# Griffin-style hybrid block on one core: operand blocks of the gates' Strassen products copied by transfers inside SBUF, and two of the sums T made by one instruction

## The chip, the cores and the metric

The kernel runs on one core of a Trainium2 chip. The metric is the device time of one execution in microseconds (us). TensorE is called PE, VectorE DVE, ScalarE ACT, GpSimd POOL; SP is the engine from whose queue most transfers are issued.

## What is computed

One layer on a stream of 512 tokens by 2048 features, in float32. The part that matters here is the gates: of the combined input projection, the last two blocks of 2048 columns are `gate_attn` and `gate_conv`, whose sigmoids weigh the attention and the convolution branch.

```
    u = rms_norm(h, mix_pre_g[l])
    proj = u @ w_in[l]
    q, k, v, ca, cb, ga, gb = jnp.split(proj, split_pts, axis=-1)
    ...
    merged = jax.nn.sigmoid(ga) * y_attn + jax.nn.sigmoid(gb) * y_conv
    h = h + rms_norm(merged @ w_out[l], mix_post_g[l])
```

## The kernel before

Tokens lie along the free dimension (NT = 512), features on the 128 partitions; the 2048 features of `u` are 16 tiles of 128x512. Each float32 operand is held as a rounded high part and a low rest (`un0h`, `un0l` and so on), and a product is the sum of three matmuls: high by low, high by high, low by high.

The stages run in program order: convolution inputs, values, queries and keys with attention (8 heads), the gates, layer norm, the output projections, then the feed-forward part. PE, ACT, DVE, POOL and SP each have a queue that is worked in order; a scheduler fixed that order when the kernel was built, and waits between the queues are semaphores.

The gates have 16 output tiles each. The first two of each come by plain products: the loop over `c` (0 to 7) takes one weight chunk of 128x1024 (`raw_g0_c`, split by ACT into `whi_g0_c`, line 124, and by DVE into `wlo_g0_c`, line 125) and issues 24 matmuls (lines 534 to 536) into the four PSUM banks `g0_0` to `g0_3`. The other 14 come by Strassen's scheme with Winograd's sums (`strassen`), which needs other operands: the blocks `b` of `u` (feature tile `c` for "11", tile `c + 8` for "21" and "22"), high part beside low part in one tile of 128x512, and the four sums T1 to T4, again as high beside low. The same loop over `c` makes them, beside the matmuls:

- `un` (line 537): high plus low of feature tile `c` on POOL and of tile `c + 8` on DVE, 128x512 each, into one buffer `un{c}`.
- `b` (lines 542 and 543): per `c` three blocks; the high half of each is copied by ACT, the low half by POOL, 128x256 each. That is 24 copies on ACT and 24 on POOL.
- `tt` (lines 192 to 195, `winograd_t`): the four sums on DVE, 128x256 each. T2 (line 193) needs T1 (line 192), T4 (line 195) needs T2.
- `t12`, `t34` (lines 146 and 147, `merged`): the high part of each sum on ACT, the low part on DVE, four pairs per `c`.

`un` and `tt` share a pool of two buffers, taken in turn. So `un{c+1}` starts when the last sum of `c` (line 195) has been read out of `un{c}`, and `tt{c+1}` starts when all four pairs of `c` are done. The blocks and sums go into a pool of 66 slots of 128x512, in which the slots of finished tiles are used again.

After the loop ACT loads the sigmoid's table and applies it to the four banks (line 555). The first Strassen product, `g2`, accumulates in the bank that the first sigmoid sets free (line 237, then line 239), with `b00` to `b07` as its moving operand. Its weights (`g2q`, `g2s`, `g3q`, `g3s`, lines 217 and 250) are loaded through SP's queue; a weight buffer is loaded anew when DVE has read it, so SP waits for `wlo_g0_4` to `wlo_g0_7` in between.

Of the kernel before, what the change touches and what calls it, by code (L numbers as in the profile page):

```python
# [25 lines left out]
F32 = mybir.dt.float32  # L26
F32R = mybir.dt.float32r
AF = mybir.ActivationFunctionType
ALU = mybir.AluOpType
# [33 lines left out]
def hybrid_block(ctx: ExitStack, tc, xT, vecs, rpb, mask, w_c0, w_qk, w_v, w_gg, w_cg, w_ao, w_co, w_out, w_g0, w_gu, w_dn, outT):  # L63
    nc = tc.nc
# [12 lines left out]
    A, B = slice(0, HN), slice(HN, NT)  # L77

    def slot(name, dt=F32, shape=(P, NT)):
        return sp.tile(list(shape), dt, tag="slot", name=name)  # L80
# [35 lines left out]
    def wchunk(src, name, parts=1):  # L116
        w = src.shape[-1]
        raw = wp.tile([P, 1024], F32, tag="raw", name=f"raw_{name}", bufs=6)[:, :w]
        hi = wp.tile([P, 1024], F32R, tag="whi", name=f"whi_{name}")[:, :w]
        lo = wp.tile([P, 1024], F32R, tag="wlo", name=f"wlo_{name}")[:, :w]  # L120
        for n in range(parts):
            s = slice(n * w // parts, (n + 1) * w // parts)
            nc.sync.dma_start(raw[:, s], src[:, s])
            nc.scalar.copy(hi[:, s], raw[:, s])  # L124
            nc.vector.tensor_tensor(out=lo[:, s], in0=raw[:, s], in1=hi[:, s].bitcast(F32), op=ALU.subtract)  # L125
        taps(rate)
        return hi, lo
# [15 lines left out]
    def merged(src, name):  # L143

        t = slot(name, F32R)
        nc.scalar.copy(t[:, A], src)
        nc.vector.tensor_tensor(out=t[:, B], in0=src, in1=t[:, A].bitcast(F32), op=ALU.subtract)
        return t
# [41 lines left out]
    def winograd_t(u1, u2, t12, t34):  # L190

        nc.vector.tensor_tensor(out=t12[:, A], in0=u1[:, B], in1=u1[:, A], op=ALU.subtract)
        nc.vector.tensor_tensor(out=t12[:, B], in0=u2[:, B], in1=t12[:, A], op=ALU.subtract)
        nc.vector.tensor_tensor(out=t34[:, A], in0=u2[:, B], in1=u1[:, B], op=ALU.subtract)
        nc.vector.tensor_tensor(out=t34[:, B], in0=u2[:, A], in1=t12[:, B], op=ALU.subtract)

    def operands(b11, b2, t12, t34):
        return {
            "11": b11,
            **{n: [t[i] for t in b2] for i, n in enumerate(("21", "22"))},  # L200
            **{n: [t[i] for t in t12] for i, n in enumerate(("T1", "T2"))},
            **{n: [t[i] for t in t34] for i, n in enumerate(("T3", "T4"))},
        }
# [203 lines left out]
    un = []  # L407
# [20 lines left out]
    for half in range(2):  # L428
        rate = R_V[half]
        pv = [(bank, abank)[half](f"pv{half}_{t}") for t in range(NB)]  # L430
        for c in range(HT):
# [3 lines left out]
            for k in range(2):  # L435
                s = slice(k * NT, (k + 1) * NT)
                kt = c * 2 + k
                ah, al = u[kt]
# [88 lines left out]
    for c in range(HT):  # L527
        hi, lo = wchunk(w_gg[c], f"g0_{c}")
        un = stp.tile([P, 2, NT], F32, tag="S", name=f"un{c}")
        for j, k in enumerate((c, c + HT)):  # L530
            ah, al = u[k]
            for n, ps in enumerate(pg):
                s = slice((j * 4 + n) * P, (j * 4 + n + 1) * P)
                nc.tensor.matmul(ps, hi[:, s], al, start=c + j == 0, stop=False)
                nc.tensor.matmul(ps, hi[:, s], ah, start=False, stop=False)
                nc.tensor.matmul(ps, lo[:, s], ah, start=False, stop=c + j == HT)
            (nc.gpsimd, nc.vector)[j].tensor_tensor(
                out=un[:, j], in0=ah.bitcast(F32), in1=al.bitcast(F32), op=ALU.add
            )
            blocks = [slot(f"b{j}{c}_{n}", F32R) for n in range(1 + j)]  # L540
            for t, cols in zip(blocks, (A, B)):
                nc.scalar.copy(t[:, A], ah[:, cols].bitcast(F32))
                nc.gpsimd.tensor_copy(t[:, B], al[:, cols].bitcast(F32))
            if j:
                b2.append(blocks)
            else:
                b11.append(blocks[0])
        tt = stp.tile([P, 2, NT], F32, tag="S", name=f"tt{c}")
        winograd_t(un[:, 0], un[:, 1], tt[:, 0], tt[:, 1])
        t12.append([merged(tt[:, 0, cols], f"t12{c}_{n}") for n, cols in enumerate((A, B))])  # L550
        t34.append([merged(tt[:, 1, cols], f"t34{c}_{n}") for n, cols in enumerate((A, B))])
    for i in range(2):
# [10 lines left out]
    op = operands(b11, b2, t12, t34)  # L563
# [69 lines left out]
    f, acc = [], None  # L633
# [38 lines left out]
    for c in (*range(SPLIT), *range(HT)):  # L672
        if len(w) == c:
            w.append(wchunk(w_g0[0, c], f"f0_{c}"))
            u += [(slot(f"u2_{i}h", F32R), slot(f"u2_{i}l", F32R)) for i in (2 * c, 2 * c + 1)]
            cols = A if c < SPLIT else slice(0, NT)
        else:
            cols = B
# [12 lines left out]
    for j in range(3):  # L691
        t = stp.tile([P, 2, NT], F32, tag="S", name=f"sg{j}")
        t, up = t[:, 0], t[:, 1]
# [10 lines left out]
    for c in range(HT):  # L704
        hi, lo = wchunk(w_g0[1, c], f"f1_{c}")
        for k in range(2):
            i = 2 * c + k
            nc.vector.scalar_tensor_tensor(out=f[i], in0=f[i], scalar=col(C_FPRE, i), in1=r3, op0=ALU.mult, op1=ALU.mult)
            if i < HT:
                moving = [merged(f[i][:, cols], f"b1{i}_{n}") for n, cols in enumerate((A, B))]  # L710
                b11.append(moving[0])
            else:
                moving = [merged(f[i][:, cols], f"b2{i}_{n}") for n, cols in enumerate((A, B))]
                b2.append(moving)
            for n in range(4):
                s = slice((k * 4 + n) * P, (k * 4 + n + 1) * P)
                for m, cols in enumerate((A, B)):
                    plain(pf[n][:, cols], hi[:, s], lo[:, s], moving[m], i + m == 0, i == KT - 1)
            if i >= HT:
                t12, t34 = slot(f"t12_{i}"), slot(f"t34_{i}")  # L720
                winograd_t(f[i - HT], f[i], t12, t34)
                b_t12.append([merged(t12[:, cols], f"t12{i}_{n}") for n, cols in enumerate((A, B))])
                b_t34.append([merged(t34[:, cols], f"t34{i}_{n}") for n, cols in enumerate((A, B))])
    for j in range(2):
        t = slot(f"sg{3 + j}")
# [5 lines left out]
    op = operands(b11, b2, b_t12, b_t34)  # L731
# [6 lines left out]
    for j in range(5, FT):  # L738
# [5 lines left out]
        t, up = slot(f"sg{j}"), slot(f"su{j}")  # L744
# [53 lines left out]
    for i in range(0, KT - 4, 4):  # L798
        t = stp.tile([P, 4, HN], F32, tag="S" if i else "S1", name=f"ha{i}")
        nc.gpsimd.dma_start(t, h_d[i : i + 4, :, A].rearrange("k p t -> p k t"))  # L800
        ha += [t[:, m] for m in range(4)]
    for i in range(KT - 4, KT, 2):
        t = stp.tile([P, 2, HN], F32, tag="quad", name=f"ha{i}", bufs=3)
# [111 lines left out]
```

## Time and profile before

| | |
|---|---|
| median of 3 runs | 2588.96 us (2587.96 to 2590.28) |
| the profiled execution: its time | 2587.58 us |
| the profiled execution: its span | 2585.8 us |
| mean granted clock of TensorE | 0.991 |
| DVE busy in the span | 68% |
| ACT busy in the span | 42% |
| POOL busy in the span | 10% |
| last matmul of the last head's attention starts | 496.63 us |
| the 8 turns of the loop over `c` on DVE (line 195 of turn 0 to line 195 of turn 7) | 496.4 to 540.0 us |
| first matmul of the first Strassen product | 542.58 us |

A row of the time line has the start in us, the duration in us, the engine, line, operation, tile written and tiles read, the count, and in brackets the idle time before it with what ended it. Durations include the pipeline's tail: DVE instructions of 128x256 that follow each other closely last 0.41 to 0.42 us but start 0.33 to 0.34 us apart. [...]

### The profile page before, as it was taken

Reading aid. Unit: us, or ns where it says so; the run is one execution under the profiler, and the core shown is the slowest. Engines: PE = TensorE matmul, PEld = TensorE weight load, DVE = VectorE, ACT = ScalarE, POOL = GpSimd, SP = SyncE. Lnnn points to the kernel's source line nnn. Section 1 sums busy time; section 2 is a strip of 40 time slices with the busy share of each in tenths; the row PEclk is TensorE's granted clock in tenths of the full one; section 3 lists DMA queues with packets and bytes.
Section 4 is the critical chain, followed back from the end, with each engine's and each line's share of the span. In section 5 each row is a group of like instructions: output and inputs, shape, how many; then the busy total and the mean of one; then the engine's idle time right before and its main releaser. Section 6 shows DMA issues by size and latency. Waiting matters only on the chain.

```text
span 2585.8 us, 33614 instructions
## 1 busy us (share of the span) xinstructions
PE 2535.4 (98%) x13078; PEld 2168.7 (84%) x13078; DVE 1751.2 (68%) x2224; ACT 1079.6 (42%) x1560; POOL 263.9 (10%) x290
## 2 busy tenths in 40 slices
PE   9999999989999999998999999999999999999996
PEld 8888888778888888887998888888888878888886
DVE  5999896687776655338888888888788832233336
ACT  5223333455554422224555555555555532233222
POOL 0110222320000011004100000000000100010003
PEclk9999999989999999999999999999999999999998
DMA  6234323356667435234356656656655653353334
GB/s 215 93 127 148 108 95 104 109 149 189 184 189 251 143 129 189 95 104 151 107 158 182 173 172 180 179 171 173 185 169 168 206 174 103 94 170 98 96 97 136
DMA packets 124624, 385.42 MB, mean 149 GB/s; under 512 B 14256, under 2 KB 21552, under 8 KB 124464
## 3 DMA queue, kind: packets, MB, share of 16 engines
q1 hardware_dynamic: 96464, 311.47, 37.0%
q0 software_dynamic: 13024, 45.62, 8.7%
q10 hardware_dynamic: 14976, 26.19, 2.8%
q8 instruction: 102, 1.67, 0.3%
q14 instruction: 58, 0.48, 0.1%
HBM read 350.72 MB, written 32.51 MB: 148 GB/s over the span
## 4 chain that ended last, share of the span: by engine, by line
PE 92%; DVE 4%; issue 2%; ACT 1%; DMA 1%; POOL 1%; POOLq 0%; DVEq 0%; ACTq 0%; SPq 0%
PE f L237 19%; PE f L239 10%; PE g L237 7%; PE pd L170 5%; PE pd L173 5%; PE pd L174 5%; PE g L239 3%; PE po L173 2%; PE po L174 2%; PE po L170 2%; PE qk L174 2%; PE qk L173 2%; PE qk L170 2%; PE py L170 2%; PE py L174 2%; PE py L173 2%
## 5 line engine op out<-in xcount | busy, mean ns | idle before, releaser
L125 DVE TENSOR_TENSOR wlo_wd<-raw_wd,whi_wd 128x1024 fp32r<-128x1024 f32 (+1 forms) x90 | 102.3, 1136 | 283.7 <-ACT whi_wd L124 283.7
L124 ACT CAST whi_wd<-raw_wd 128x1024 fp32r<-128x1024 f32 (+1 forms) x90 | 88.4, 982 | 312.8 <-PE pd L173 306.8
L376 DVE SCALAR_TENSOR_TENSOR cv<-z,vec,cv 128x497 f32<-128x497 f32 (+14 forms) x240 | 190.9, 797 | 4.7
L125 DVE TENSOR_TENSOR wlo_wo<-raw_wo,whi_wo 128x1024 fp32r<-128x1024 f32 x36 | 47.4, 1318 | 106.9 <-ACT whi_wo L124 106.9
L124 ACT CAST whi_wo<-raw_wo 128x1024 fp32r<-128x1024 f32 x36 | 37.9, 1054 | 130.0 <-PE po L173 122.7
L124 ACT CAST whi_y<-raw_y 128x1024 fp32r<-128x1024 f32 x32 | 33.5, 1052 | 78.8 <-PE py L173 75.5
L124 ACT CAST whi_qk<-raw_qk 128x1024 fp32r<-128x1024 f32 x32 | 33.6, 1051 | 77.1 <-PE qk L173 52.7
L125 DVE TENSOR_TENSOR wlo_qk<-raw_qk,whi_qk 128x1024 fp32r<-128x1024 f32 x32 | 40.4, 1261 | 32.3 <-ACT whi_qk L124 32.1
L125 DVE TENSOR_TENSOR wlo_y<-raw_y,whi_y 128x1024 fp32r<-128x1024 f32 x32 | 52.2, 1634 | 10.7 <-ACT whi_y L124 9.5
L616 DVE TENSOR_TENSOR gg<-py,gg 128x512 f32<-128x512 f32 x32 | 21.8, 690 | 53.1 <-PE py L174 53.1
L294 POOL TENSOR_TENSOR r_r<-r_v,mhalf 128x2 f32<-128x2 f32 (+1 forms) x6 | 7.7, 1283 | 458.2 <-DVE r_v L292 458.2
L735 POOL DMA_DIRECT2D ad<-a_d x44 | 24.0, 555 | 262.4 <-PE pd L170 197.6
L170 PE MATMUL py<-ycl,whi_y 128*128 128x512 f32 x128 | 49.8, 389 | 0.0
L173 PE MATMUL py<-ych,whi_y 128*128 128x512 f32 x128 | 49.8, 389 | 0.0
L174 PE MATMUL py<-ych,wlo_y 128*128 128x512 f32 x128 | 49.8, 389 | 0.0
L747 ACT ACTIVATE sg<-sg 128x512 f32<-128x512 f32 x39 | 24.7, 634 | 50.2 <-DVE sg L275 50.2
L455 POOL TENSOR_TENSOR bm<-braw,msk 128x128 f32<-128x128 f32 x56 | 43.0, 801 | 14.0 <-DMA braw<-in_rpb 13.9
L153 PE MATMUL f<-b,whi_f 128*128 128x256 f32 x128 | 36.2, 283 | 0.0
L154 PE MATMUL f<-b,wlo_f 128*128 128x256 f32 x128 | 36.2, 283 | 0.0
L152 PE MATMUL f<-b,whi_f 128*128 128x256 f32 x128 | 36.2, 283 | 0.0
L626 POOL TENSOR_TENSOR gg<-gg,gg 128x512 f32<-128x512 f32 x16 | 21.7, 1355 | 111.2 <-ACT whi_y L124 69.6
L124 ACT CAST whi_ca<-raw_ca 128x1024 fp32r<-128x1024 f32 x12 | 12.6, 1053 | 47.2 <-PE cb L173 19.0
(3045 smaller groups left out, 8284.4 us busy)
## 6 DMA issues: line engine op xcount, KB each, us to landing
raw_wd<-in_w_dn SPq DMA_DIRECT2D x60, 512.0 KB, 3.5
raw_wo<-in_w_out SPq DMA_DIRECT2D x36, 512.0 KB, 3.8
raw_qk<-in_w_qk SPq DMA_DIRECT2D x32, 512.0 KB, 3.7
raw_wd<-in_w_dn SPq DMA_DIRECT2D x30, 384.0 KB, 3.1
a_d<-sg ACTq DMA_DIRECT2D x44, 256.0 KB, 3.7
ad<-a_d POOLq DMA_DIRECT2D x44, 256.0 KB, 4.8
raw_v<-in_w_v SPq DMA_DIRECT2D x16, 512.0 KB, 4.4
raw_y<-in_w_ao SPq DMA_DIRECT2D x16, 512.0 KB, 3.7
```

What stands on the lines that cost most here:

```text
L124: nc.scalar.copy(hi[:, s], raw[:, s])
L125: nc.vector.tensor_tensor(out=lo[:, s], in0=raw[:, s], in1=hi[:, s].bitcast(F32), op=ALU.subtract)
L152: nc.tensor.matmul(o, hi, t[:, B], start=first, stop=False, skip_group_check=True)
L153: nc.tensor.matmul(o, hi, t[:, A], start=False, stop=False, skip_group_check=True)
L154: nc.tensor.matmul(o, lo, t[:, A], start=False, stop=last, skip_group_check=True)
L170: mmul = nc.tensor.matmul(ps, hi[:, s], al, start=first, stop=False)
L173: nc.tensor.matmul(ps, hi[:, s], ah, start=False, stop=False)
L174: nc.tensor.matmul(ps, lo[:, s], ah, start=False, stop=last)
L237: nc.tensor.matmul(ps, hi[:, ws[k]], t, start=first and k == 0, stop=False, skip_group_check=True)
L239: nc.tensor.matmul(ps[:, A], lo[:, ws[k]], t[:, A], start=False, stop=last and k == HT - 1, skip_group_check=True)
L376: nc.vector.scalar_tensor_tensor(out=a[:, to], in0=z[:, fr], scalar=col(C_WDW, i * CW + w), in1=a[:, to], op0=ALU.mult, op1=ALU.add)
L455: nc.gpsimd.tensor_tensor(out=bm[:, o + i - i0], in0=raw[:, :, i * BC : (i + 1) * BC], in1=msk[:, o + i - i0, None, :].broadcast_to([P, RO ...
```

## The change

In the gates' stage, the 48 copies into the blocks `b` are no longer instructions of ACT and POOL but transfers from SBUF to SBUF, issued from SP, 128x256 float32 (128 KB) each. The tile is allocated as float32 and read as `F32R` afterwards. T1 and T3 are made by one DVE instruction of 128x2x256 (`winograd_tt`, line 200 of the changed kernel), T2 and T4 as before (lines 201 and 202). The second place where the four sums are made (the feed-forward stage) keeps `winograd_t`.

```
+    def winograd_tt(un, tt):
+
+        left = un.rearrange("p k (h t) -> p (k h) t", h=2)
+        nc.vector.tensor_tensor(out=tt[:, :, A], in0=left[:, 1::2], in1=left[:, 0:2], op=ALU.subtract)
+        nc.vector.tensor_tensor(out=tt[:, 0, B], in0=un[:, 1, B], in1=tt[:, 0, A], op=ALU.subtract)
+        nc.vector.tensor_tensor(out=tt[:, 1, B], in0=un[:, 1, A], in1=tt[:, 0, B], op=ALU.subtract)
...
-            blocks = [slot(f"b{j}{c}_{n}", F32R) for n in range(1 + j)]
+            blocks = [slot(f"b{j}{c}_{n}") for n in range(1 + j)]
             for t, cols in zip(blocks, (A, B)):
-                nc.scalar.copy(t[:, A], ah[:, cols].bitcast(F32))
-                nc.gpsimd.tensor_copy(t[:, B], al[:, cols].bitcast(F32))
+                nc.sync.dma_start(t[:, A], ah[:, cols].bitcast(F32))
+                nc.sync.dma_start(t[:, B], al[:, cols].bitcast(F32))
+            blocks = [t.bitcast(F32R) for t in blocks]
...
-        winograd_t(un[:, 0], un[:, 1], tt[:, 0], tt[:, 1])
+        winograd_tt(un, tt)
```

The order of PE's instructions is the same in both kernels. On the other engines the order moves in this stage alone. Lines from 196 on have numbers higher by 7 in the changed kernel up to the copies (537 is 544, 542 and 543 are 549 and 550), and by 8 behind them.

On DVE, in turns 0 and 1 (`t120` and `t340` are the pairs of turn 0, `t121` and `t341` those of turn 1), before:

```order
L537 TENSOR_TENSOR un1_4111<-un9h_1608,un9l_1609 128x512
L147 TENSOR_TENSOR t120_0_4093<-tt0_4088,t120_0_4093 128x256
L147 TENSOR_TENSOR t120_1_4096<-tt0_4088,t120_1_4096 128x256
L147 TENSOR_TENSOR t340_0_4099<-tt0_4088,t340_0_4099 128x256
L147 TENSOR_TENSOR t340_1_4102<-tt0_4088,t340_1_4102 128x256
L192 TENSOR_TENSOR tt1_4147<-un1_4111 128x256
L194 TENSOR_TENSOR tt1_4147<-un1_4111 128x256
L193 TENSOR_TENSOR tt1_4147<-un1_4111,tt1_4147 128x256
L195 TENSOR_TENSOR tt1_4147<-un1_4111,tt1_4147 128x256
L125 TENSOR_TENSOR wlo_g0_4_4284<-raw_g0_4_4282,whi_g0_4_4283 128x1024
```

and in the changed kernel:

```order
L544 TENSOR_TENSOR un1_4110<-un9h_1608,un9l_1609 128x512
L125 TENSOR_TENSOR wlo_g0_4_4280<-raw_g0_4_4278,whi_g0_4_4279 128x1024
L147 TENSOR_TENSOR t120_0_4092<-tt0_4088,t120_0_4092 128x256
L147 TENSOR_TENSOR t120_1_4095<-tt0_4088,t120_1_4095 128x256
L147 TENSOR_TENSOR t340_0_4098<-tt0_4088,t340_0_4098 128x256
L147 TENSOR_TENSOR t340_1_4101<-tt0_4088,t340_1_4101 128x256
L200 TENSOR_TENSOR tt1_4146<-un1_4110 128x2x256
L201 TENSOR_TENSOR tt1_4146<-un1_4110,tt1_4146 128x256
L147 TENSOR_TENSOR t121_0_4150<-tt1_4146,t121_0_4150 128x256
L202 TENSOR_TENSOR tt1_4146<-un1_4110,tt1_4146 128x256
```

The rest of weight chunk 4 has moved ahead of the pairs of turn 0 and with it, on ACT, the cast that it waits for.

On POOL, around turn 3, before:

```order
L537 TENSOR_TENSOR un3_4229<-un3h_1282,un3l_1283 128x512
L543 CAST b03_0_4243<-un3l_1283 128x256
L543 CAST b13_0_4259<-un11l_1656 128x256
L543 CAST b13_1_4260<-un11l_1656 128x256
L537 TENSOR_TENSOR un4_4288<-un4h_1508,un4l_1509 128x512
```

and in the changed kernel:

```order
L544 TENSOR_TENSOR un3_4226<-un3h_1282,un3l_1283 128x512
L544 TENSOR_TENSOR un4_4284<-un4h_1508,un4l_1509 128x512
L544 TENSOR_TENSOR un5_4342<-un5h_1514,un5l_1515 128x512
L544 TENSOR_TENSOR un6_4400<-un6h_1555,un6l_1556 128x512
L544 TENSOR_TENSOR un7_4458<-un7h_1561,un7l_1562 128x512
```

Nothing but the `un` sums is left on POOL from turn 2 to turn 7.

On SP, the queue of transfers, in the changed kernel (`g3q` are the weights of the second Strassen tile; before, no other transfer stood between them):

```order
L224 DMA g3q_4712<-in_w_cg 128x1024
L549 DMA b04_0_4298<-un4h_1508 128x256
L550 DMA b04_0_4298<-un4l_1509 128x256
L549 DMA b14_0_4314<-un12h_1696 128x256
L550 DMA b14_0_4314<-un12l_1697 128x256
L549 DMA b14_1_4315<-un12h_1696 128x256
L550 DMA b14_1_4315<-un12l_1697 128x256
L549 DMA b05_0_4356<-un5h_1514 128x256
L550 DMA b05_0_4356<-un5l_1515 128x256
L549 DMA b15_0_4372<-un13h_1702 128x256
L550 DMA b15_0_4372<-un13l_1703 128x256
```

The 48 transfers stand behind `g3s` in the queue: 12, then the third `g2q`, 6, the fourth `g2q`, 6, the first `g3q`, 12, the second `g3q`, 12, and then the last two `g3q`.

## The prediction

> **What bounds the kernel now.** I read the page first, then the list of PE's waits in the gates' stage, the busy times by stretch, and the time line of each engine there.
>
> ```profile
> span 2585.8 us, 33614 instructions
> PE 92%; DVE 4%; issue 2%; ACT 1%; DMA 1%; POOL 1%; POOLq 0%; DVEq 0%; ACTq 0%; SPq 0%
> ```
>
> PE carries 92% of the chain that ended last, so the change, which touches no matmul, can only act where PE waits. In the window of the gates' loop the list of waits (engine, line, waited for: us, times, longest) has four:
>
> ```profile
> PE g L237 <- ACT gs L555: 4.6, 1, 4.6
> PE g L536 <- DVE wlo_g L125: 4.0, 1, 4.0
> PE g L237 <- ACT g2h L232: 1.6, 1, 1.6
> PE po L501 <- DVE ptl L499: 1.1, 1, 1.1
> ```
>
> The first is the end of the loop: PE has finished its plain products and waits for the first sigmoid to free a bank. The second is in mid-loop: the rest of weight chunk 5 comes late from DVE. They look like two gains, but are one. The rows of PE show the pace:
>
> ```profile
> 514.98 0.39 PE L535 MATMUL g<-un5h,whi_g 128*128 128x512 f32 x1
> 519.36 0.80 PE L536 MATMUL g<-un5h,wlo_g 128*128 128x512 f32 x1 [3.99 <-DVE wlo_g L125]
> 526.91 0.39 PE L534 MATMUL g<-un6l,whi_g 128*128 128x512 f32 x1
> 532.35 0.39 PE L534 MATMUL g<-un7l,whi_g 128*128 128x512 f32 x1
> 542.58 2.90 PE L237 MATMUL g<-b,g2h 128*128 128x512 f32 x6 [4.63 <-ACT gs L555]
> ```
>
> One turn is 24 matmuls in 532.35 - 526.91 = 5.44 us, 0.227 us each. Without the wait at 515 the 70 matmuls that are left would end at 515.2 + 70 x 0.227 = 531.1 instead of 537.9, and PE would then wait longer for the same sigmoid. So the start of `g2` at 542.58 is set by what leads to that sigmoid, and that is the loop on DVE with POOL's `un` and ACT's casts:
>
> ```profile
> core 0: us, PE busy (x) PEld busy (x) DVE busy (x) ACT busy (x) POOL busy (x), PEclk, DMA share, GB/s
> 496.39:540.03 43.64, 37.57 (x155) 30.31 (x153) 39.37 (x70) 23.70 (x61) 29.29 (x34) 0.92 0.33 89
> 538.00:542.60 4.60, 0.02 (x1) 0.05 (x1) 4.60 (x11) 3.53 (x7) 0.00 (x0) 0.89 0.01 2
> 540.54 1.28 ACT L555 ACT_TABLE_LOAD   x1
> 541.84 1.09 ACT L555 ACTIVATE gs<-g 128x512 f32<-128x512 f32 x2
> ```
>
> From the last sum of turn 0 to that of turn 7 DVE is busy 39.4 of 43.6 us: it is the bound of the loop. Behind it stand the last casts, the table load (1.28) and one sigmoid, a tail of 542.58 - 540.03 = 2.55 us that the change leaves as it is.
>
> **Why DVE is that busy.** Its instructions are stretched:
>
> ```profile
> L147 DVE TENSOR_TENSOR t<-tt,t 128x256 fp32r<-128x256 f32 x32 | 19.6, 655 | 1.7 <-ACT t L146 1.7
> L147 DVE TENSOR_TENSOR t<-tt,t x32: 411/418/2122, 498.8 to 540.6; 128x256 fp32r<-128x256 f32 x32
> L194 DVE TENSOR_TENSOR tt<-un 128x256 f32<-128x256 f32 x8 | 3.7, 465 | 0.0
> L195 DVE TENSOR_TENSOR tt<-un,tt 128x256 f32<-128x256 f32 x8 | 3.3, 417 | 0.0
> ```
>
> The same shape takes 411 ns at best and 655 ns in the mean of line 147: 32 x 0.244 = 7.8 us lost there alone, and about 1.4 more in lines 192 to 194. What runs on POOL meanwhile tells the cause:
>
> ```profile
> 498.21 0.39 POOL L543 CAST b<-un0l 128x256 fp32r<-128x256 f32 x1
> 498.85 3.34 DVE L147 TENSOR_TENSOR t<-tt,t 128x256 fp32r<-128x256 f32 x4 [1.74 <-ACT t L146]
> 513.10 0.58 DVE L192 TENSOR_TENSOR tt<-un 128x256 f32<-128x256 f32 x1 [1.18 <-POOL un L537]
> 513.35 1.13 POOL L543 CAST b<-un11l 128x256 fp32r<-128x256 f32 x2
> 514.68 0.41 DVE L147 TENSOR_TENSOR t<-tt,t 128x256 fp32r<-128x256 f32 x1
> 515.35 1.82 DVE L147 TENSOR_TENSOR t<-tt,t 128x256 fp32r<-128x256 f32 x2
> 515.57 1.32 POOL L537 TENSOR_TENSOR un<-un4h,un4l 128x512 f32<-128x512 f32 x1 [1.09 <-DVE tt L195]
> ```
>
> Beside three casts (513.0 to 514.5) three DVE sums take 514.68 - 513.10 = 1.58 us where 3 x 0.33 = 1.0 would do: 0.6 us for three casts, 0.2 each. Beside `un4` two instructions of line 147 take 1.82 instead of 0.75. A cast takes 0.39 us where DVE is idle (498.21) and 0.57 here. So the two engines hold each other up, casts and `un` alike.
>
> **The change part by part.**
>
> The 24 casts on POOL go. Each costs DVE between 0.2 us (the stretch at 513) and 0.39 us (all of a cast's own time), so 4.8 to 9.4 us in all. The four at 498.85 lose 3.34 - 4 x 0.34 = 2.0 us beside five casts, but transfers are prepared on POOL then too, and that stays. I take 0.25, near the lower row, since nothing else runs there: 24 x 0.25 = **6.0 us** off the loop.
>
> [...]
>
> T1 and T3 in one instruction: 256 more columns in the same instruction save the fixed part. The rows of DVE for 128x512 and 128x256 give it:
>
> ```profile
> 502.29 0.43 DVE L192 TENSOR_TENSOR tt<-un 128x256 f32<-128x256 f32 x1
> 502.63 0.42 DVE L194 TENSOR_TENSOR tt<-un 128x256 f32<-128x256 f32 x1
> 511.24 0.68 DVE L537 TENSOR_TENSOR un<-un11h,un11l 128x512 f32<-128x512 f32 x1
> ```
>
> Two of 256 end after 0.34 + 0.42 = 0.76 us, one of 512 after 0.68: 8 x 0.08 = **0.6**, say 0.5, off the loop (bounds 0 and 0.6).
>
> The 24 copies on ACT go: ACT is busy 23.7 of 43.6 us, so it is not the bound, and this is worth nothing but at one place. Before 498.85 DVE waits 1.74 us for the first cast of turn 0, which stands behind three copies (0.9 us) on ACT:
>
> ```profile
> 497.49 0.41 ACT L542 CAST b<-un0h 128x256 fp32r<-128x256 f32 x1
> 497.96 0.40 PE L535 MATMUL g<-un9h,whi_g 128*128 128x512 f32 x1
> 500.56 1.05 ACT L124 CAST whi_g<-raw_g 128x1024 fp32r<-128x1024 f32 x1
> 523.85 1.22 DVE L125 TENSOR_TENSOR wlo_g<-raw_g,whi_g 128x1024 fp32r<-128x1024 f32 x1
> ```
>
> In the new order the cast of weight chunk 4 (1.05 us) takes their place; it must wait for the last matmul that reads its buffer (497.96 + 0.40), so DVE goes on at 498.36 + 1.05 = 499.4 and waits 2.3 us: **0.5 us** on the loop (bounds -0.9, the copies alone, and +0.8). In exchange the rests of chunks 5 to 7 come earlier in DVE's order, and PE's wait at 515 goes. This is worth nothing, as shown: the cover is the wait for the sigmoid, which then grows from 4.6 to about 5.5 us. If the loop became shorter than PE's 531.1, the 4 us would count.
>
> The 48 transfers are new work for SP. The nearest rows are the stores of the same shape out of SBUF at the kernel's end, and loads that are issued in a run:
>
> ```profile
> L820 SPq DMA_DIRECT2D out<-y x16: 332/386/403, 2551.9 to 2563.6; - x16
> DMA to landing us min/median/max: 1.7/1.8/1.8
> L87 SPq DMA_DIRECT2D xr<-in_xT x16: 327/354/814, 1000.9 to 1012.1; - x16
> 492.31 0.42 SPq L250 DMA_DIRECT2D g3s<-in_w_cg x1
> ```
>
> At 0.39 us of SP each, 48 are 18.5 us from 492.7 on, with waits in between for the rests of chunks 4 to 7, since weight loads stand among them. The last 12 stand behind the load that waits for chunk 7's rest, made until 525.0 now (the row at 523.85) and earlier in the new order: 525.0 + 12 x 0.39 + 1.8 = 531.5 at the latest. PE reads the blocks from 536 on, so 5 us of slack cover them. Queued behind them on SP are the third and fourth `g2q` and the `g3q`, which serve products behind the first. The pairs of the later turns take slots that the transfers read; those have landed by then. Cost 0; what it costs if the cover is gone is the last rival.
>
> Sum: -6.0 - 0.5 + 0.5 = **-6.0 us**. The profiled execution of 2587.58 (span 2585.8 and 1.8 around it) would become 2581.6; it lies 1.4 under the median of the runs, so the median goes from 2588.96 to **2583.0**. Behind the loop PE has no wait that could take this up: `g2` starts at about 536.6, at the same half clock as now, and the 1.6 us wait behind the first product stays.
>
> **The rivals.**
>
> *The casts were no load.* DVE is stretched by `un` alone, and where the casts stretched it, `un` and the waits for it (1.18 us at 513.10) grow into the room. The row at 515.35, stretched with no cast beside it, speaks for this, the stretch at 513 against it, as no `un` runs there. Then the merged instruction and the longer wait at 497 are all, -0.5 + 0.5: 2589.0.
>
> *The casts cost their whole length.* 24 x 0.39 = 9.4, so -9.4 - 0.5 + 0.5 = -9.4: 2579.6. The 498.85 row (0.4 per cast) speaks for it; the stretch at 513 against it. [...]
>
> *SP's queue is too slow.* One mechanism: SP works in order, and if one transfer within SBUF holds it longer than the 0.39 us of the rows, the block `b07`, the 43rd of 48, comes late to the eighth matmul of `g2`, which now starts at 536.6 + 3.0 = 539.6. It decides from (539.6 - 1.8 - 492.7) / 43 = 1.05 us per transfer. At 1.3 us (between the row and the 1.8 us of a landing, were each to wait for the one before) `b07` lands at 492.7 + 43 x 1.3 + 1.8 = 550.4, 4.8 us after the 545.6 of now: 2593.8. For it: no row shows a copy within SBUF. Against it: the issue takes 0.33 to 0.42 us in every row, whatever the tile.
>
> **How the numbers follow.** Forecast 0.55 (2580.5 to 2586), no load 0.20, whole length 0.13, slow queue 0.12. The range 2579 to 2589 leaves out the slow queue and a little below; the likeliest case's own is the one in brackets. A measurement here can tell about 0.2%, 5.2 us, from no change, so faster means under 2583.8. The forecast's own bounds straddle that: 0.42 of its 0.55 counts as faster, with the 0.13 of the whole length 0.55; 0.13 + 0.20 = 0.33 within; 0.12 slower.
>
> **What would show it.** Right: line 147 in this stage at a mean of about 500 ns, still stretched where `un` runs; the sums of turn 7 end near 534; no wait of PE for `wlo_g`, the wait for the first sigmoid over 5 us; the first matmul of `g2` near 536.6; SP done with the blocks before 532. Wrong: line 147 still above 600 ns (no load), a wait of PE at `g2` for a DMA (slow queue), or DVE idle more than before because POOL's `un` has become the longer path.

## The result, and the profile after

| | before | changed |
|---|---|---|
| median of 14 runs each, us | 2588.23 (2585.49 to 2590.28) | 2583.23 (2581.37 to 2586.20) |
| ratio, 95% interval | | 0.9982 [0.9974, 0.9991] |
| span of the profiled execution, us | 2585.8 | 2582.3 |
| last of the four sums of turn 7 ends | 540.03 | 536.98 |
| first matmul of `g2` | 542.58 | 539.42 |
| first matmul of `g3` | 566.52 | 562.40 |

The change makes the kernel 5.0 us faster (2.3 to 6.7 by the interval). That is close to the forecast of 2583.0, but the profile shows a gain of another make: `g2` starts 3.2 us earlier, not 6.0, and the span is 3.5 us shorter. (The profiled execution of the kernel before, 2587.58 us, lies 0.65 under its median, that of the changed one, 2584.07, lies 0.84 above; this makes the 3.5 out of 5.0.)

The fourth part of the page (each engine's share of the chain), then PE's wait for the first sigmoid in the gates' stage (engine, line, waited for: us, times, longest), of the changed kernel:

```profile
PE 94%; DVE 2%; issue 1%; ACT 1%; DMA 1%; POOL 0%; SPq 0%; POOLq 0%; DVEq 0%; ACTq 0%
PE g L244 <- ACT gs L563: 8.0, 1, 8.0
```

DVE's share of the chain fell from 4% to 2%. The wait for `wlo_g` in mid-loop is gone, and the wait for the first sigmoid grew from 4.6 to 8.0. PE's time line:

```profile
531.06 0.39 PE L543 MATMUL g<-un15h,wlo_g 128*128 128x512 f32 x1
539.42 3.55 PE L244 MATMUL g<-b,g2h 128*128 128x512 f32 x8 [7.97 <-ACT gs L563]
```

PE now ends its plain products at 531.06 + 0.39 and then stands for 8 us, so all of the stage is bound by what leads to the sigmoid. The loop from the sum of turn 0 to that of turn 7 (columns: PE, PEld, DVE, ACT, POOL busy, clock, DMA share, GB/s), and the groups of DVE in the stage:

```profile
496.56:536.97 40.41, 34.89 (x155) 28.61 (x153) 36.97 (x64) 16.48 (x37) 13.35 (x10) 0.98 0.85 258
L147 DVE TENSOR_TENSOR t<-tt,t 128x256 fp32r<-128x256 f32 x30 | 17.9, 636 | 0.1
L200 DVE TENSOR_TENSOR tt<-un 128x512 f32<-128x512 f32 x8 | 5.5, 690 | 1.8 <-POOL un L544 1.2
499.73 1.23 DVE L125 TENSOR_TENSOR wlo_g<-raw_g,whi_g 128x1024 fp32r<-128x1024 f32 x1 [2.44 <-ACT whi_g L124]
536.56 0.42 DVE L202 TENSOR_TENSOR tt<-un,tt 128x256 f32<-128x256 f32 x1
```

POOL is busy 13.4 us where it was 29.3, with 10 instructions where it had 34, and ACT 16.5 where it was 23.7. Yet DVE is still busy 37.0 of 40.4 us: it is the bound as before, and line 147 still has a mean of 636 ns over the 30 in this window (622 over all 32, which was 655 before) where 410 is what it takes undisturbed. The transfers, by the summary for line 549:

```profile
DMA to landing us min/median/max: 2.0/4.2/7.4
```

Each holds SP for about 0.6 us (0.46 to 1.83) and lands 4.2 us after its issue in the median. PE waits for none of them.

### The profile page after: what moved, and what is told of

Same layout as the page of the kernel before. It is cut to its first block, busy times and chain, and to the rows that moved or that the text cites. A ratio compares the mean times of both kernels' runs of the same rounds, so it can differ in the third digit from the quotient of the medians.

```text
span 2582.3 us, 33652 instructions
## 1 busy us (share of the span) xinstructions
PE 2531.9 (98%) x13078; PEld 2166.5 (84%) x13078; DVE 1749.6 (68%) x2216; ACT 1072.2 (42%) x1536; POOL 248.0 (10%) x266
## 4 chain that ended last, share of the span: by engine, by line
PE 94%; DVE 2%; issue 1%; ACT 1%; DMA 1%; POOL 0%; SPq 0%; POOLq 0%; DVEq 0%; ACTq 0%
PE f L244 19%; PE f L246 10%; PE g L244 7%; PE pd L170 5%; PE pd L173 5%; PE pd L174 5%; PE g L246 4%; PE po L174 2%; PE po L170 2%; PE po L173 2%; PE qk L174 2%; PE qk L173 2%; PE qk L170 2%; PE py L170 2%; PE py L174 2%; PE py L173 2%
## 5 line engine op out<-in xcount | busy, mean ns | idle before, releaser
L491 ACT ACTIVATE sc<-sc,st 128x256 f32<-128x256 f32 (+1 forms) x32 | 18.0, 563 | 33.0 <-DVE st L490 33.0
```

## The experiments

The changed kernel has three parts: the low halves leave POOL, the high halves leave ACT, and T1 and T3 are one instruction. The theory was that DVE is slowed by POOL's casts and that all of the gain is theirs. The first three kernels take the parts one by one; the others try what was left.

| kernel | median, us (runs) | ratio to before, 95% | first matmul of `g2` |
|---|---|---|---|
| low_by_transfer | 2583.35 (10) | 0.9984 [0.9975, 0.9994] | 537.39 |
| merge_only | 2590.45 (10) | 1.0011 [1.0001, 1.0020] | 543.69 |
| transfers_only | 2583.34 (10) | 0.9981 [0.9972, 0.9991] | 537.51 |
| un_on_dve | 2578.28 (5) | 0.9965 [0.9952, 0.9978] | 534.42 |
| un_on_dve_sep | 2576.81 (5) | 0.9957 [0.9943, 0.9970] | 532.91 |
| sig_early | 2575.49 (5) | 0.9951 [0.9938, 0.9963] | 529.75 |
| before_un_on_dve | 2582.93 (11) | 0.9979 [0.9970, 0.9987] | 537.29 |
| high_by_transfer | 2587.62 (10) | 0.9997 [0.9988, 1.0006] | 544.66 |
| b11_ahead | 2578.93 (6) | 0.9967 [0.9955, 0.9980] | 529.86 |

### low_by_transfer: POOL's casts alone

Against the kernel before, the line of the low halves only (the type of the tile is handled as in the change):

```diff
-                nc.gpsimd.tensor_copy(t[:, B], al[:, cols].bitcast(F32))
+                nc.sync.dma_start(t[:, B], al[:, cols].bitcast(F32))
```

> Only the low halves of the blocks go by transfer; ACT's copies and the four separate sums stay, and the order on DVE and ACT is that of the kernel before. Theory A (POOL's casts hold DVE up for part of their length): lines 192 to 194 fall from 465 to 484 ns to about 415, the sum of turn 7 ends near 537, the first matmul of g2 starts at 539 to 540.5 us (542.58 before, 539.42 with the change), ratio about 0.9988. Theory B (the time DVE loses to POOL only moves from the casts to `un`; what gained was the new order): g2 at 542 to 543, ratio 1.000.

Its groups of DVE in the stage, and the first four pairs of line 147:

```profile
L147 DVE TENSOR_TENSOR t<-tt,t 128x256 fp32r<-128x256 f32 x32 | 15.3, 519 | 1.8 <-ACT t L146 1.8
L192 DVE TENSOR_TENSOR tt<-un 128x256 f32<-128x256 f32 x8 | 3.4, 422 | 4.9 <-POOL un L544 4.7
498.87 1.43 DVE L147 TENSOR_TENSOR t<-tt,t 128x256 fp32r<-128x256 f32 x4 [1.77 <-ACT t L146]
```

Line 147 falls from 655 to 519 ns, line 192 to the undisturbed 422, and the pairs at 498.87 take 1.43 us where they took 3.34. The order on DVE is that of the kernel before, so the lengths can be set side by side: line 147 is 32 x 0.136 = 4.4 us shorter in all, lines 192 to 194 1.3, the rest 0.8, together 6.4 us or 0.27 for each of the 24 casts. In return DVE waits 4.7 us for POOL's `un` where it waited 3.5, and 5.2 us are left: `g2` starts at 537.39, 5.2 us or 0.22 a cast earlier than before, and earlier than the 539 to 540.5 that was expected. The whole gain of the change is there in this one line, without its other two parts. The casts were the load.

### merge_only: T1 and T3 in one instruction, nothing else

Against the kernel before:

```diff
-        winograd_t(un[:, 0], un[:, 1], tt[:, 0], tt[:, 1])
+        winograd_tt(un, tt)
```

> Only T1 and T3 in one instruction. Theory A: about 0.5 us, g2 at 542.1, ratio 0.9998. Rival (the merged instruction with its new order carries the gain): g2 at or under 541.

`g2` comes 1.1 us later than before and the time is 0.1% longer (1.0001 to 1.0020): the merged instruction is a loss. PE's wait for `wlo_g` shrank from 4.0 to 1.3 us and the wait for the sigmoid grew by 6.1, to 10.7: once more the first of the two waits is worth nothing.

### transfers_only: the change without the merge

Against the changed kernel:

```diff
-        winograd_tt(un, tt)
+        winograd_t(un[:, 0], un[:, 1], tt[:, 0], tt[:, 1])
```

> Only the 48 transfers; four separate sums. Theory A: most of the gain, g2 at 539.7 to 540.2, ratio about 0.9985. Rival (the merged instruction carries it): g2 at 541 or later.

With separate sums `g2` starts at 537.51, so in the change the merge costs 539.42 - 537.51 = 1.9 us there. That is also earlier than expected (539.7 to 540.2), as the merge had been counted as a gain. Beside low_by_transfer (537.39) it shows that taking ACT's copies away as well adds nothing in the sum. Why the merge costs is to be read in turn 1, first of transfers_only, DVE and then ACT:

```profile
502.21 0.43 DVE L192 TENSOR_TENSOR tt<-un 128x256 f32<-128x256 f32 x1
502.55 0.42 DVE L194 TENSOR_TENSOR tt<-un 128x256 f32<-128x256 f32 x1
502.89 0.42 DVE L193 TENSOR_TENSOR tt<-un,tt 128x256 f32<-128x256 f32 x1
503.56 0.42 DVE L195 TENSOR_TENSOR tt<-un,tt 128x256 f32<-128x256 f32 x1
502.67 0.41 ACT L146 CAST t<-tt 128x256 fp32r<-128x256 f32 x1 [1.94 <-DVE tt L192]
```

and of the changed kernel:

```profile
502.40 0.69 DVE L200 TENSOR_TENSOR tt<-un 128x512 f32<-128x512 f32 x1
503.13 0.43 DVE L201 TENSOR_TENSOR tt<-un,tt 128x256 f32<-128x256 f32 x1
503.57 0.42 DVE L147 TENSOR_TENSOR t<-tt,t 128x256 fp32r<-128x256 f32 x1
503.91 0.42 DVE L202 TENSOR_TENSOR tt<-un,tt 128x256 f32<-128x256 f32 x1
503.13 1.17 ACT L146 CAST t<-tt 128x256 fp32r<-128x256 f32 x3 [2.20 <-DVE tt L200]
```

From the first sum to the last one the separate order takes 503.56 - 502.21 = 1.35 us, the merged one 1.51, though it has one instruction less. In the separate order T3 (line 194), which needs nothing of T1, stands between T1 and T2, and every instruction starts 0.34 us after the one ahead. Merged, T2 (line 201) stands right behind the instruction that makes its input and starts 0.73 us after it, when that has ended. And T1 is there only when T3 is too, at 503.09 rather than 502.64: ACT's cast of it starts 0.46 us later, and line 147, the low part of the same sum, waits for it and starts 0.44 us after line 201 instead of 0.34. A third gap does not show in turn 1. Line 192 (T1) reads only the half of `un` that POOL has made; the merged instruction, which makes T3 as well, also reads the half that DVE has made just ahead of it. In the changed kernel, then in transfers_only:

```profile
512.24 0.68 DVE L544 TENSOR_TENSOR un<-un11h,un11l 128x512 f32<-128x512 f32 x1
513.02 0.69 DVE L200 TENSOR_TENSOR tt<-un 128x512 f32<-128x512 f32 x1
513.62 1.22 DVE L125 TENSOR_TENSOR wlo_g<-raw_g,whi_g 128x1024 fp32r<-128x1024 f32 x1
```

```profile
517.23 0.68 DVE L544 TENSOR_TENSOR un<-un12h,un12l 128x512 f32<-128x512 f32 x1
517.83 0.41 DVE L192 TENSOR_TENSOR tt<-un 128x256 f32<-128x256 f32 x1
```

The merged instruction starts 0.78 us after that `un`, line 192 only 0.60 after it; this comes in four turns. (Line 125, which needs nothing of line 200, starts 0.60 us behind it: it is the need that makes the gap, not the form of the merged instruction.) From start to start over the seven turns, the gaps between `un` and line 200, lines 200 and 201, and lines 201 and 147 add 0.7, 0.7 and 0.4 us, and the merged instructions save 0.5. With 0.2 us in turn 0, and one pair of turn 7 (0.34) that stands ahead of the last sum in the changed kernel and behind it in transfers_only, that is 1.8 of the 1.9 us. POOL's `un` has next to no part in it: it stretches the pairs 2.2 us more in the changed kernel (line 147 at 622 ns over all 32, against 552), but transfers_only has two waits for `un` there, of 1.19 and 1.15 us, which the changed kernel has not.

### un_on_dve: POOL's last work in the loop, too

Against the changed kernel:

```diff
-            (nc.gpsimd, nc.vector)[j].tensor_tensor(
+            nc.vector.tensor_tensor(
```

> The change, and the eight `un` sums of POOL on DVE too, so that POOL does nothing beside the loop. Theory C (what is left of DVE's stretching comes from POOL's `un`, about 1.1 us in each turn): line 147 falls from a mean of 636 ns to about 415; DVE's own work from turn 0 to turn 7 is 14 x 0.61 + 7 x 1.28 + 28 x 0.34 + 5 x 1.14 = 32.7 us, with 2.4 us of wait at the start it ends near 531.5, g2 at about 534, ratio to before about 0.9965. Rival (the hand-overs between ACT and DVE bound the loop, and `un` on DVE is simply more work): g2 at 539 or later, ratio 0.998 or above.

What still stretched line 147 in the changed kernel is POOL's `un`; of the changed kernel, turn 2, then of un_on_dve:

```profile
510.12 2.20 DVE L147 TENSOR_TENSOR t<-tt,t 128x256 fp32r<-128x256 f32 x3
510.34 1.35 POOL L544 TENSOR_TENSOR un<-un3h,un3l 128x512 f32<-128x512 f32 x1 [4.53 <-DVE tt L202]
```

```profile
L147 DVE TENSOR_TENSOR t<-tt,t 128x256 fp32r<-128x256 f32 x32 | 12.1, 419 | 0.1
531.56 0.42 DVE L202 TENSOR_TENSOR tt<-un,tt 128x256 f32<-128x256 f32 x1
```

Three pairs beside one `un` take 2.20 us where 1.08 would do. With eight instructions of 0.6 us more on DVE the loop's last sum still comes 5.0 us earlier (531.56 against 536.56): line 147 runs at a mean of 419 ns, and the waits for `un` are gone. The wait for `un0` at 493.94 (1.2 us) goes too; it had held up the last of the attention, and without it the rest of chunk 4 waits 1.13 us instead of 2.44, so about 1.3 of the 5.0 us are won at the start of the loop. Giving POOL this work was a loss in the kernel before as in the changed one.

### un_on_dve_sep: the same with separate sums

Against un_on_dve:

```diff
-        winograd_tt(un, tt)
+        winograd_t(un[:, 0], un[:, 1], tt[:, 0], tt[:, 1])
```

> The transfers stay, the un sums of both halves run on DVE (as in un_on_dve), and the four sums are separate again. Theory (the merged instruction costs the loop by itself: the sum behind it, line 201, has to wait for it, and line 147 behind that for ACT's cast, about 0.15 us a turn): the first matmul of g2 comes 1.1 us earlier than in un_on_dve, near 533.3, and the time is near 2577.2. Rival (the merge cost only because POOL's un fell on three queued pairs of line 147, and POOL has nothing left to do here): no difference, 534.4 and 2578.3. The prediction's own step (the merge saves 0.5): 534.9 and 2578.8.

```profile
530.06 0.41 DVE L195 TENSOR_TENSOR tt<-un,tt 128x256 f32<-128x256 f32 x1
532.91 3.12 PE L244 MATMUL g<-b,g2h 128*128 128x512 f32 x8 [2.96 <-ACT gs L563]
```

The loop's last sum comes 1.5 us earlier than in un_on_dve (530.06 against 531.56) and so does `g2`. As POOL has nothing to do here, the merge costs by itself, and the rival that put it all on POOL falls. The two times cannot be told apart by their intervals; the profile can.

### sig_early: the sigmoids ahead of turn 7's sums

Against un_on_dve_sep; the lines of the sigmoids behind the loop go.

```diff
+        if c == HT - 1:
+            for i in range(2):
+                for j in range(2):
+                    sg = slot(f"gs{i}_{j}")
+                    nc.scalar.activation(sg, pg[2 * i + j], AF.Sigmoid)
+                    nc.scalar.dma_start(g_d[j * KT + i], sg)
+        for j, k in enumerate((c, c + HT)):
+            ah, al = u[k]
             nc.vector.tensor_tensor(
```

> As un_on_dve_sep, but the four sigmoids and their table load stand ahead of the un sums, the four sums and the pairs of turn 7 in the program. Theory (what leads to the first sigmoid sets the start of g2): PE ends its plain products near 529.7 and starts g2 within 2 us of it, near 531; the eighth matmul then waits for the block b07, which lands 4.2 us after its issue at 531.5, at about 535.7, against an eighth matmul at about 537.5 in un_on_dve. So the gain on un_on_dve_sep is some 2 us: near 2575. Rival (the casts of turn 7, now 3.5 us behind the sigmoids on ACT, come late to the products T1 to T4): the gain is lost in a wait of PE for t, near 2577 or above.

```profile
529.75 1.75 PE L244 MATMUL g<-b,g2h 128*128 128x512 f32 x7
534.25 0.47 PE L244 MATMUL g<-b,g2h 128*128 128x512 f32 x1 [2.75 <-DMA b<-un7l]
535.52 3.54 PE L244 MATMUL g<-t,g2h 128*128 128x512 f32 x8
```

PE goes from the plain products into `g2` without a gap, at full clock (1.00 up to 535), and then stops for the eighth block: the transfer of `b07` has become the bound. The second product starts at 535.52, against 539.14 in un_on_dve_sep, and loses a part again to the half clock (low from 535.60 to 539.02). At 2575.49 this has the lowest median of all, some 12 us under the kernel before, and its interval lies clear of the changed kernel's; it overlaps that of un_on_dve_sep, so only the profile tells these two apart.

### before_un_on_dve: the casts by themselves

The edit of un_on_dve, in the kernel before: POOL does nothing but casts in the loop.

> The kernel before with one edit: all un sums on DVE, so that POOL does nothing but its 24 casts in the loop. It measures the casts by themselves. No casts at all is un_on_dve_sep (theory: g2 near 533.3). Theory (a cast costs DVE 0.22 us): 533.3 + 5.3 = 538.6, line 147 at a mean near 480 ns, time near 2582.5. Rival 'whole length' (0.39 each): 542.7, 2586.6. Rival 'no load' (only un stretched DVE): 533.3, line 147 near 415 ns.

```profile
L147 DVE TENSOR_TENSOR t<-tt,t 128x256 fp32r<-128x256 f32 x32 | 16.1, 547 | 0.5 <-ACT t L146 0.5
502.44 5.78 DVE L147 TENSOR_TENSOR t<-tt,t 128x256 fp32r<-128x256 f32 x4
518.69 17.32 POOL L543 CAST b<-un7l 128x256 fp32r<-128x256 f32 x1 [7.74 <-DVE un L537]
534.34 0.41 DVE L195 TENSOR_TENSOR tt<-un,tt 128x256 f32<-128x256 f32 x1
```

and of un_on_dve_sep:

```profile
520.81 1.21 DVE L241 TENSOR_TENSOR g2l<-g2q,g2h 128x1024 fp32r<-128x1024 f32 x1
```

Against un_on_dve_sep, in which the sum of turn 0 starts at the same time (495.34), the last sum comes 534.34 - 530.06 = 4.3 us later. The casts cost more than that, as two things hide a part of it: the wait at the first pair is 0.49 us here against 1.15 for chunk 4's cast there, and the rest of the first weights of `g2` (`g2l`, 1.13 us from start to start) stands inside the loop there and behind it here (at 535.70). Set against their undisturbed lengths, DVE's instructions in this loop are 5.9 us longer in all. Of the 24 casts 20 ran within the loop, so this is 0.30 for each; with `g2l` in the loop `g2` would by this reckoning have come at 538.4, near the 538.6 of the theory.

It is not one price. Beside 12 casts that start from 503.32 to 507.44 four pairs take 5.78 us where 1.42 would do, about 0.35 a cast; beside the next three, at 509.18 to 510.37, three sums lose 0.6 us, 0.2 a cast. And the cast of `un7l` stood on POOL for 17.32 us, to 536.01, while DVE's instructions followed each other closely at their undisturbed lengths until the loop was over; no loss to it shows on DVE. So 'whole length' (0.39 each) falls in the sum, though the four pairs come near it, and 'no load' falls too. And this edit of one line gains as much as the whole change (0.9979 against 0.9982).

### high_by_transfer: ACT's copies alone

Against the kernel before, the line of the high halves only.

```diff
-                nc.scalar.copy(t[:, A], ah[:, cols].bitcast(F32))
+                nc.sync.dma_start(t[:, A], ah[:, cols].bitcast(F32))
```

> Only ACT's 24 copies become transfers, POOL's casts stay and the sums are separate. Theory (ACT is not the bound, its copies are worth nothing but at the first cast of turn 0): g2 between 542.1 and 543.1, time within 0.05% of the kernel before. Rival (ACT's copies hold up its casts for line 147 all along the loop, and POOL's only hid it): some us earlier, 540 or below.

```profile
498.10 2.00 DVE L147 TENSOR_TENSOR t<-tt,t 128x256 fp32r<-128x256 f32 x4 [0.85 <-ACT t L146]
537.81 0.41 DVE L195 TENSOR_TENSOR tt<-un,tt 128x256 f32<-128x256 f32 x1
539.15 1.21 DVE L241 TENSOR_TENSOR g2l<-g2q,g2h 128x1024 fp32r<-128x1024 f32 x1
541.61 1.04 ACT L239 CAST g2h<-g2s 128x1024 fp32r<-128x1024 f32 x1 [2.89 <-DVE g2s L229]
544.66 3.43 PE L244 MATMUL g<-b,g2h 128*128 128x512 f32 x8 [9.79 <-issue]
```

The time is that of the kernel before, as expected, but `g2` comes 2.1 us later, not within 542.1 to 543.1. The last sum comes 1.8 us earlier (537.81 + 0.41 against 540.03). Of this, 1.1 us is `g2l`, which stands behind the last sum here and ahead of it in the kernel before (line 234, at 533.15), and 0.9 us is the shorter wait for the first cast of turn 0 (0.85 against 1.74). So ACT's copies were worth something at that one place alone, as the theory had it. `g2` is late all the same because the scheduler put a cast of weights, which waits for a sum on DVE, ahead of the sigmoid's table load. What the edit would bring without that was not tried.

### b11_ahead: `b07` earlier in SP's queue

Against sig_early, `copied_blocks` being the same lines as a function (its text is left out here, and so is the call for turn 0 ahead of the loop):

```diff
+            if j:
+                b2.append(copied_blocks(1, c))
+            elif c + 1 < HT:
+                b11.append(copied_blocks(0, c + 1)[0])
```

> As sig_early, but the two transfers for the first product's block of turn c + 1 (b01 to b07) are issued in turn c, ahead of the four of that turn. In sig_early PE waits 2.75 us for b07, and after that the clock is at half from 535.6 to 539.0. Theory (the place of b07 in SP's queue is what bounds the start of g2 there): b07 is issued near 526 and lands near 530, PE has no wait within the first product, waits about 1 us for the cast g2h that ends near 533.7, the clock stays at 1.0, and the second product starts 1.5 to 2 us earlier than its 535.52; with the clock the gain is 2 to 3 us, near 2573. Rival (the transfers of the later turns wait for free slots or for the loads in the same queue, so that b07 lands no earlier or another block is late instead): a wait of PE for a DMA stays in the first product, and the time stays near 2575.5.

```profile
528.53 0.59 SPq L540 DMA_DIRECT2D b<-un7l  x1
529.74 3.32 ACTq L559 DMA_DIRECT2D g_d<-gs  x2
533.43 0.47 PE L244 MATMUL g<-b,g2h 128*128 128x512 f32 x1 [1.82 <-DMA b<-un7l]
538.21 3.78 PE L244 MATMUL g<-t,g2h 128*128 128x512 f32 x8 [3.36 <-ACT g2h L239]
```

A miss. `b07` is issued 1.8 us earlier than in sig_early and used only 0.8 us earlier (533.43 against 534.25). And the two stores behind the first sigmoids hold ACT for 3.32 us, where they took 0.86 in sig_early; the casts of turn 7 and `g2h` stand behind them, PE waits 3.36 us for `g2h`, and the second product starts 2.7 us later than in sig_early. Both sides of it are transfers that come slower than forecast; why the stores were held so much longer in this order stays open.

## Why the prediction was right or wrong

**What bounds the loop: right.** The two waits of PE were one gain. `wlo_g` no longer holds PE, the plain products end at 531.06 + 0.39 (531.1 was said for an undisturbed run), and the wait for the sigmoid took it over. The tail from the last sum to `g2` is 539.42 - 536.98 = 2.4 us, against 2.55.

**The casts: right in mechanism, 0.8 too large in the sum.** 0.25 us a cast was taken, 6.0 in all. What the casts took of DVE's time was more than that, 0.27 a cast (6.4 us) in low_by_transfer and 0.30 in before_un_on_dve. But without them DVE waits 1.2 us longer for POOL's `un`, a term that the sum had left out and only the rival 'no load' had named, so that 5.2 us are left. A cast takes 0.39 us by itself (498.21 in the kernel before). The traces show 0.2 to 0.35 us a cast lost on DVE, less than that, and come near it in the four pairs at 502.44 of before_un_on_dve; the pairs at 510.12 of the changed kernel lose 1.1 us beside an `un` of 1.35.

**The merged instruction: the step that failed.** Forecast -0.5 with bounds of 0 and -0.6; measured +1.9 in the change, +1.5 without POOL, +1.1 in the kernel before. The duration was right (690 ns for 512 columns against 0.34 + 0.42). What the step left out is who needs whom: the merge removed the one independent instruction that stood between a sum and the next that needs it, gave ACT its first sum 0.46 us later, and made T1 wait for the half of `un` that DVE makes just ahead. These gaps add 1.8 us in the change, where the shorter instruction saves 0.5. A loss was not among the bounds because only lengths were added up.

**The wait at 497: right.** +0.5 was said, a wait of 2.3 us and DVE going on at 499.4; it is 2.44 us and 499.73, of which 0.2 us is that the stage began later.

**ACT's copies are worth nothing but at the first cast of turn 0: right.** In the change they add nothing (537.51 against 537.39), and alone 0.9 us at that cast (high_by_transfer), which is the bound that was given.

**The transfers cost nothing: right, with wrong durations.** 0.39 us of SP each was taken from stores and loads, and 1.8 us to land; it is 0.6 and 4.2. (Nor did every row have an issue of 0.33 to 0.42, as was said: the loads of line 87 go up to 0.81.) The last one is issued at 533.15, where all were to have landed by 531.5, and the slack still covers it: the price stayed under the 1.05 us from which that rival decided. With `g2` 10 us earlier, in sig_early, the same transfers are what PE waits for. The rival was the right one to name; only the start of `g2` decides it.

**Behind the loop: wrong on two counts.** "At the same half clock as now" was not so. PE's clock by the microsecond, of the kernel before and then of the changed one:

```profile
541.00:542.00 1.00, 0.00 (x0) 0.00 (x0) 1.00 (x2) 0.99 (x2) 0.00 (x0) 0.81 0.03 8
548.00:549.00 1.00, 0.04 (x1) 0.00 (x0) 0.00 (x0) 0.93 (x2) 0.00 (x0) 0.78 0.99 391
```

```profile
535.00:536.00 1.00, 0.00 (x0) 0.00 (x0) 0.91 (x2) 0.22 (x1) 0.00 (x0) 0.87 0.00 0
542.00:543.00 1.00, 1.00 (x5) 0.77 (x5) 0.00 (x0) 0.00 (x0) 0.00 (x0) 0.72 1.09 209
```

Between these rows the clock is at 0.5. A slice at 0.81 holds 0.38 us of half clock, one at 0.78 holds 0.44; so it is low from 541.62 to 548.44 before, and from 535.74 to 542.56 now, 6.8 us in both. Before, `g2` ran in 5.9 of them; now in 3.1, as PE still waits when the low stretch begins. That brings about 1 us on top: `g3` starts 4.1 us earlier where `g2` starts 3.2 earlier. And behind the gates PE does have waits that move: the one for `ya4l`, of before, changed and transfers_only:

```profile
830.49 0.50 PE L170 MATMUL py<-ya4l,whi_y 128*128 128x512 f32 x1 [1.55 <-DVE ya4l L135]
825.59 0.50 PE L170 MATMUL py<-ya4l,whi_y 128*128 128x512 f32 x1 [1.23 <-DVE ya4l L135]
825.61 0.79 PE L170 MATMUL py<-ya4l,whi_y 128*128 128x512 f32 x1 [2.46 <-DVE ya4l L135]
```

At 826 the changed kernel is 4.9 us ahead of the kernel before, and 1.4 us of this are gone by the end, about as much as the wait for `u_5l` in the feed-forward stage has grown (from 0.3 to 1.9). transfers_only is 1.9 us ahead of the change at `g2` and 1.2 at `g3`, and here the lead is gone, in a wait that is 1.2 us longer; this fits the one median of the two. What sets the length of these two waits was not tried.

**So the time was in part luck.** At `g2` the terms make -5.2 for the casts, +1.9 for the merge, and the rest (the wait at 497, ACT's copies, the start of the stage) next to nothing, where -6.0 was forecast; the clock, which the sum took as unchanged, gave back 1 us. The measured 5.0 us, with its interval of 2.3 to 6.7, cannot tell 6.0 from 3.5. The median before is 0.7 us lower over 14 runs than over the three from which 2583.0 was reckoned, and that brought the two times closer still. Of the rivals, 'no load' falls with low_by_transfer, 'whole length' with the 0.27 and 0.30 us a cast, and 'slow queue' did not come into play.

## What to carry to other kernels

When an engine is slowed by another one at work beside it, as DVE here by POOL (0.27 to 0.30 us a cast), ask first whether the second should have the work at all: moving `un` from POOL to DVE, busy for 39.4 of the loop's 43.6 us, gained as much as 48 transfers did (0.9979 against 0.9982). Before two instructions become one, look at what stood between a producer and its consumer, and who waits for the first half: an instruction less can be a longer chain. Before two loops are compared by their ends, see that the same instructions stand in both: `g2l`, inside one loop and behind the other, is 1.1 us in two of the comparisons here. A wait that is hidden is hidden only from where the next bound lies: each step that brought `g2` forward here (the casts, the sums, the sigmoid) uncovered the next.

## What the runs showed of the hardware

- TensorE's clock fell to half behind the plain products, for 6.8 us in the kernel before, in the changed one, in transfers_only and in b11_ahead, and for 3.4 in un_on_dve_sep, after a wait of 3.0 us, and in sig_early, after one of 2.75. In merge_only and high_by_transfer, after waits of 10.7 and 9.8, the first eight matmuls of `g2` took 3.75 and 3.43 us, where eight in `g3` took 2.00. Here are the first and the last slice of sig_early, low from 535.60 to 539.02:

```profile
535.00:536.00 1.00, 1.00 (x8) 0.90 (x7) 1.00 (x2) 1.00 (x2) 0.00 (x0) 0.80 0.59 197
539.00:540.00 1.00, 1.00 (x10) 1.00 (x9) 0.14 (x1) 0.91 (x1) 0.00 (x0) 0.99 0.84 234
```

  In the first six of these traces it began 3.7 to 4.9 us after PE first stopped behind the plain products, in un_on_dve_sep (533.72) and sig_early (535.60) with PE at work again, from 532.91 and 534.25.
- A transfer of 128 KB within SBUF held SP for about 0.6 us in a run of them, against medians of 0.35 and 0.39 us for the loads of line 87 and the stores of line 820 in the profile before, and landed after 4.2 us in the median (2.0 to 7.4 for those of line 549 in the changed kernel).
- A cast of 128x256 on POOL cost DVE 0.27 us in the mean of low_by_transfer and 0.30 in before_un_on_dve, from about 0.2 beside single sums to 0.35 beside four pairs, of its own 0.39. One such cast stood on POOL for 17.32 us while DVE's instructions followed each other at their undisturbed lengths (518.69 in before_un_on_dve). An addition of 128x512 on POOL, of 1.35 us, cost three DVE instructions beside it 1.1 us.
- On DVE an instruction that needed the result of the one ahead started when that had ended (0.73 us after the start of a 128x512 sum: 502.40 and 503.13 in the changed kernel), while an independent one started 0.60 us after the start of such a sum (506.02 and 506.62, 513.02 and 513.62 in the changed kernel). For sums of 128x256 it was 0.45 against 0.34 us (501.08 and 501.53 in low_by_transfer).
